# A decoder block on one core: sums, diagonals and transposes regrouped, the first values' weights loaded in halves, and another order of the end

## The chip, the cores and the metric

The kernel runs on one core of a Trainium2 chip. The metric is the device time of one execution in microseconds (us). Before the change three runs took 449.29, 447.87 and 447.54 us, a median of 447.87.

## The reference, cut to what matters

A block for 256 tokens of width 1024: a norm, one wide projection (latents of queries, 384, and of keys and values, 256; one rotary key; queries, keys and values of eight further heads; two gates), two attentions of eight heads, their merge, an output projection, a gated MLP with a convolution over three tokens, and a final norm.

```python
h = rmsnorm(x, attn_norm[l])
proj = h @ w_in[l]
q_lat, kv_lat, k_pe, qkv_b = ...
q = rmsnorm(q_lat, q_norm[l]) @ w_uq[l]
kv = rmsnorm(kv_lat, kv_norm[l]) @ w_ukv[l]
y_a = causal_attention_blocks(q_a, k_a, v_a, ...) @ w_o_mla[l]
y_b = moba_attention(rope(qkv[0], pos), rope(qkv[1], pos), qkv[2]) @ w_o_moba[l]
x = x + (g_a * y_a + g_b * y_b) @ w_out[l]
h = rmsnorm(x, ffn_norm[l])
u = causal_dwconv(h @ w_up[l], conv_w[l], conv_b[l])
x = x + (silu(u[..., :D_FF]) * u[..., D_FF:]) @ w_down[l]
return rmsnorm(x, final_norm)
```

## The kernel before, in words

**Products.** Every float32 operand of a large product is split into a high part (rounded to a shorter format, on ScalarE) and a low part (the rest, on VectorE), and a product is three: high times high, high times low, low times high (`mm3`, line 341; `split`, line 346). A few small products use plain float32: transposes against the identity, rows of a norm's factors, sums over partitions.

**Weights.** They come in units of 128 x 2048 (1 MB) in the order of `PLAN` (line 44). `weights` (line 353) takes the next of three raw tiles, three high and three low ones, loads the unit on SP's queue in one transfer, and splits it in two cuts of 1024 columns. A raw tile is loaded again when VectorE's subtraction has read it.

**Order.** All work is first recorded by `Program` (line 144) and then emitted by a list scheduler (`emit`, line 212): with prices per instruction (`price`, line 283) it goes on in model time, and each engine takes, of the instructions whose inputs are there, the one recorded first. SP takes its transfers strictly in recorded order. What is recorded inside `P.together()` stays in one block. So where a line stands in the program is its priority, and the order that comes out on each engine is fixed; on the chip each engine works it off in that order. From line 916 on VectorE, ScalarE and GpSimd keep the recorded order.

**Start.** Four units hold the tokens and the weights of the latents (line 510). Then the values' projection for the first 512 columns (`proj_tokens`, line 463; banks `v0`), while x is loaded again and its squares give the first norm's factor r1 (line 540, three small GpSimd operations with a power). `to_rows` (line 439) lays a factor per token out as a row in all partitions: VectorE multiplies the identity by the factor (a diagonal, from a ring of two tiles) and TensorE multiplies it by ones. `keep_values` (line 551) scales the values by r1. The second half of the values (banks `v1`, line 570) has the sums of the latents' squares (`lat_sums`, line 562) between its groups of products. Then the values' second half is kept, GpSimd works out the latents' factors `r_lat` (line 572), two `to_rows` lay them out, and the latents are scaled (line 584).

**Attentions.** Four units with two heads each of the one kind (line 663), then four of the other (line 724), with the gates' units between them. In `attention` (line 603): scores, maximum, exponentials with their sums, reciprocal; then for each head two scalings on ScalarE, three transposes in a block, a split of the transposed weights, and the products with the values.

**MLP and end.** `up_unit` (line 808) uses the second norm's factor, laid out by `to_rows` in the first unit (line 821). `down` (line 849) adds products into five banks (`parts`, line 842: for the first 128 tokens two halves of 512 columns, for the second 512, 256 and 256). The end (lines 916 to 933): `add` adds a bank to the residual and squares it on ScalarE into a column of `means`; `sum_up` adds these columns one by one, on GpSimd but for the last, which VectorE adds; `root` takes the power on GpSimd; `gains` multiplies by the final norm's weights on VectorE; `scaled` multiplies by the root in pieces and stores them, the last piece on ScalarE and its queue, the others on VectorE and SP's queue.

Of the kernel before, what the change touches and what calls it, by code (L numbers as in the profile page):

```python
# [27 lines left out]
D = 1024  # L28
# [278 lines left out]
def hybrid_block(ctx: ExitStack, tc: tile.TileContext, x, par, con, fnorm, wpack, out):  # L307
# [45 lines left out]
    def weights(kind, i, *cuts):  # L353
# [6 lines left out]
        sp.dma_start(raw[:, :n], wpack[u, :, :n])  # L360
# [76 lines left out]
    diag = Ring("diag", 2, [128])  # L437

    def to_rows(o, col2):

        for tt in range(2):
            dg = diag()
            dve.tensor_scalar(dg, ident, col2[:, tt : tt + 1], None, op0=ALU.mult)
            mm(o[:, 128 * tt : 128 * tt + 128], ones, dg, True, True, False)
# [18 lines left out]
    def proj_tokens(kind, i0, o, ah, al, *between):  # L463

        for part in range(2):
            wv = groups(weights(kind, i0 + part), 4, 512)
            for k4 in range(4):
# [6 lines left out]
                if k < len(between):  # L474
                    between[k]()
# [66 lines left out]

    rbc, c1, s1 = (T(t, [S]) for t in ("rbc", "c1", "s1"))
    p = sc_bank()
    to_rows(p[:, 0:S], r1)
# [14 lines left out]
    lat_ss = sc_bank()  # L560

    def lat_sums(j, tt):

        mm(lat_ss[:, 2 * j + tt : 2 * j + tt + 1], sq[:, 3 * j, 128 * tt : 128 * tt + 128],
           ones[:, 0:1], True, True)

    v1 = [mm_bank(), mm_bank()]
    for j, f in ((0, 1), (0, 2), (3, 4)):
        dve.tensor_add(sq[:, j], sq[:, j], sq[:, f])
    proj_tokens("v", 2, v1, xh, xl, *(partial(lat_sums, j, tt) for j in range(2) for tt in range(2)))  # L570
    keep_values(v1, 1)
# [8 lines left out]
    for j in range(2):  # L580
        to_rows(p[:, S * j : S * j + S], r_lat[:, 2 * j : 2 * j + 2])
# [18 lines left out]
    exps = T("e", [768])  # L600
    phs, pls = (Ring(t, 2, [384], F32R) for t in ("ph", "pl"))

    def attention(i, q, k, more, scale, vh, vl, yh, yl):
# [31 lines left out]
        o = av_bank()  # L635
        for hh in heads:
# [4 lines left out]
            p = sc_bank()  # L641
            with P.together():
                for b, t in enumerate((e[0][:, hh], e[1][:, hh, :128], e[1][:, hh, 128:])):
                    pe.transpose(p[:, 128 * b : 128 * b + 128], t, ident)
            ph, pl = phs(), pls()
            split(ph, pl, p[:, :384])
# [161 lines left out]
    def up_unit(i, ph, pl):  # L808
# [10 lines left out]
        if i == 0:  # L819
            p = sc_bank()  # L820
            to_rows(p[:, 0:S], r2)
            act.copy(rbc2, p[:, 0:S])
# [53 lines left out]
    def sum_up(engine, j, other):  # L876

        engine.tensor_scalar(means[:, j : j + 1], means[:, j : j + 1], other, None, op0=ALU.add)
# [4 lines left out]
    def scaled(tt, cuts):  # L883

        r = r3[:, tt : tt + 1]
        for q, (a, b) in enumerate(zip(cuts, cuts[1:])):
            if q < len(cuts) - 2:
# [81 lines left out]
```

## Time and profile before

| what | us |
|---|---|
| median of three runs | 447.87 |
| the profiled execution's own time | 447.01 |
| span of the profile, first to last instruction | 445.2 |
| TensorE busy | 435.9 |
| VectorE busy | 357.7 |
| ScalarE busy | 273.0 |
| GpSimd busy | 10.5 |

In the profile PE is TensorE, PEld its weight loads, DVE VectorE, ACT ScalarE, POOL GpSimd and SP the engine that issues most transfers (SPq, ACTq: the queues). Products overlap in TensorE's pipeline, so a product's own duration is longer than the distance of two starts. Nearly every instruction has line 246, where the program emits it, so instructions are told apart by tile: `mm`, `sc` and `av` are banks, `whi` and `wlo` the split weights, `smalls` the small columns, `B` the output tile at the end, `gate` the residual there (and, at the start, the latents), `tb` the scratch of the squares, `e` the exponentials.

### The profile page before, as it was taken

Reading aid. Unit: us, or ns where it says so; the run is one execution under the profiler, and the core shown is the slowest. Engines: PE = TensorE matmul, PEld = TensorE weight load, DVE = VectorE, ACT = ScalarE, POOL = GpSimd, SP = SyncE. Lnnn points to the kernel's source line nnn. Section 1 sums busy time; section 2 is a strip of 40 time slices with the busy share of each in tenths; the row PEclk is TensorE's granted clock in tenths of the full one; section 3 lists DMA queues with packets and bytes.
Section 4 is the critical chain, followed back from the end, with each engine's and each line's share of the span. In section 5 each row is a group of like instructions: output and inputs, shape, how many; then the busy total and the mean of one; then the engine's idle time right before and its main releaser. Section 6 shows DMA issues by size and latency. Waiting matters only on the chain.

```text
span 445.2 us, 8253 instructions
## 1 busy us (share of the span) xinstructions
PE 435.9 (98%) x3366; PEld 415.2 (93%) x3366; DVE 357.7 (80%) x553; ACT 273.0 (61%) x471; POOL 10.5 (2%) x25
## 2 busy tenths in 40 slices
PE   8999999999999999999999999999999999999993
PEld 6988999999999999999998899999999999999982
DVE  5669998798879886993788569998787797797765
ACT  5687547455735676788665658765565565565523
POOL 0012000000000000000000010000000000000003
PEclk9999999999999999999999999999999999999998
DMA  7986655435452443240479355386555555556002
GB/s 285 392 337 219 255 188 191 160 125 188 162 181 98 153 173 113 94 191 3 176 301 343 125 190 187 105 299 209 193 205 194 197 198 201 193 200 227 2 0 94
DMA packets 12997, 81.77 MB, mean 184 GB/s; under 512 B 1568, under 2 KB 2208, under 8 KB 4256
## 3 DMA queue, kind: packets, MB, share of 16 engines
q1 hardware_dynamic: 12528, 80.85, 50.4%
q8 instruction: 26, 0.43, 0.4%
q10 hardware_dynamic: 432, 0.40, 0.3%
q14 instruction: 11, 0.09, 0.1%
HBM read 80.20 MB, written 1.05 MB: 182 GB/s over the span
## 4 chain that ended last, share of the span: by engine, by line
PE 89%; DVE 4%; DMA 3%; ACT 1%; issue 1%; POOL 1%; SPq 0%; POOLq 0%; ACTq 0%; DVEq 0%
PE mm L246 63%; PE sc L246 13%; PE av L246 13%; DMA raw<-in_wpack 3%; DVE wlo L246 2%; POOL smalls L246 1%; DVE gate L246 1%; DVE VL L246 1%; ACT whi L246 0%; SPq L246 0%; DVE B L246 0%; ACT tb L246 0%; POOLq L964 0%; DVE tb L246 0%; ACT VH L246 0%
## 5 line engine op out<-in xcount | busy, mean ns | idle before, releaser
L246 DVE TENSOR_TENSOR wlo<-raw,whi 128x1024 fp32r<-128x1024 f32 (+4 forms) x155 | 175.7, 1147 | 36.1 <-ACT whi L246 35.6
L246 ACT CAST whi<-raw 128x1024 fp32r<-128x1024 f32 (+3 forms) x153 | 151.2, 1000 | 85.0 <-PE mm L246 65.7
L246 PE MATMUL mm<-XH,whi 128*128 128x256 f32 x656 | 176.9, 279 | 0.0
L246 PE MATMUL mm<-XL,whi 128*128 128x256 f32 x656 | 175.1, 277 | 0.0
L246 PE MATMUL mm<-XH,wlo 128*128 128x256 f32 x656 | 175.0, 276 | 0.0
L246 PEld LDWEIGHTS mm<-XH,whi 128*128 128x128 f32 x656 | 120.6, 188 | 1.1 <-ACT whi L246 0.6
L246 PEld LDWEIGHTS mm<-XL,whi 128*128 128x128 f32 x656 | 120.6, 188 | 0.4
L246 PEld LDWEIGHTS mm<-XH,wlo 128*128 128x128 f32 x656 | 120.4, 188 | 0.0
L246 DVE SCALAR_TENSOR_TENSOR tb<-ta,prm,tb 128x255 f32<-128x255 f32 x88 | 40.4, 480 | 2.2 <-ACT tb L246 0.7
L246 ACT ACTIVATE tb<-ta,prm 128x256 f32<-128x256 f32 x44 | 24.2, 594 | 3.8 <-DVE ta L246 3.8
L246 PE MATMUL sc<-whi,ql 128*128 128x512 f32 (+1 forms) x66 | 23.4, 355 | 0.0
L246 PE MATMUL sc<-wlo,qh 128*128 128x512 f32 (+1 forms) x66 | 23.3, 353 | 0.0
L246 PE MATMUL sc<-whi,qh 128*128 128x512 f32 (+1 forms) x66 | 23.1, 351 | 0.0
L246 ACT ACTIVATE e<-sc,smalls 128x128 f32<-128x128 f32 (+1 forms) x32 | 13.3, 420 | 12.8 <-DVE smalls L246 11.9
L246 ACT CAST qh<-ta 128x256 fp32r<-128x256 f32 (+1 forms) x26 | 11.3, 435 | 12.4 <-DVE ta L246 12.4
L246 DVE TENSOR_TENSOR ta<-ta,tb 128x256 f32<-128x256 f32 (+1 forms) x35 | 16.9, 484 | 2.2 <-ACT ta L246 0.7
L246 DVE TENSOR_TENSOR ta<-mm,rbc 128x512 f32<-128x512 f32 x22 | 15.2, 689 | 4.2 <-PE mm L246 4.2
L246 PE MATMUL mm<-YBH,whi 128*128 128x256 f32 x64 | 18.1, 283 | 0.0
L246 PE MATMUL mm<-YBH,wlo 128*128 128x256 f32 x64 | 17.7, 277 | 0.0
L246 PE MATMUL mm<-VH,whi 128*128 128x256 f32 x64 | 17.7, 277 | 0.0
L246 PE MATMUL mm<-YBL,whi 128*128 128x256 f32 x64 | 17.7, 277 | 0.0
L246 PE MATMUL mm<-VH,wlo 128*128 128x256 f32 x64 | 17.7, 276 | 0.0
(169 smaller groups left out, 741.8 us busy)
## 6 DMA issues: line engine op xcount, KB each, us to landing
raw<-in_wpack SPq DMA_DIRECT2D x66, 1024.0 KB, 4.8
raw<-in_wpack SPq DMA_DIRECT2D x7, 512.0 KB, 7.2
raw<-in_wpack SPq DMA_DIRECT2D x4, 832.0 KB, 4.2
B<-in_x SPq DMA_DIRECT2D x1, 1024.0 KB, 9.7
gate<-in_x SPq DMA_DIRECT2D x1, 1024.0 KB, 4.8
cst<-in_con SPq DMA_DIRECT2D x1, 641.0 KB, 10.7
raw<-in_wpack SPq DMA_DIRECT2D x2, 256.0 KB, 3.2
gate<-in_fnorm SPq DMA_DIRECT2D x1, 512.0 KB, 5.5
```

The costliest lines, as they stand in the source:

```text
L246: getattr(getattr(self.nc, e), method)(*args, **kw)
```

## The change

- `weights` can load a unit in several transfers. The first unit of the values is loaded in two halves and split in cuts that end at 512, 1024 and 2048.
- `to_rows` is divided: `to_diag` makes the diagonals, in six places of the tile of the exponentials (`exps`, allocated earlier) instead of a ring of two, and `to_rows` only multiplies them by ones.
- The sums of the latents' squares move from between the groups of the values' second half to one block with the rows of r1, ahead of them.
- All four diagonals of the latents' factors are multiplied in one block, recorded before the values' second half is kept. The second norm's two rows are in one block as well.
- In `attention` the transposes of both heads stand in one block behind all four scalings, and both splits come ahead of both products with the values.
- At the end all sums are GpSimd's. The last piece of the first 128 tokens is stored on SP's queue instead of ScalarE's. Of the second 128 tokens, columns 640 to 1024 and 0 to 256 are weighted ahead of the root; columns 256 to 640 get weight and root in one instruction.

```diff
--- before.py
+++ after.py
@@ -350,14 +349,16 @@
 
     units = iter(range(len(PLAN)))
 
-    def weights(kind, i, *cuts):
+    def weights(kind, i, *cuts, loads=1):
 
         u = next(units)
         assert PLAN[u] == (kind, i), (PLAN[u], kind, i)
         n = SIZE.get(kind, UNIT)
         raw, hi, lo = raws(), his(), los()
         cuts = cuts or (n // 2, n)
-        sp.dma_start(raw[:, :n], wpack[u, :, :n])
+        for j in range(loads):
+            c = slice(n * j // loads, n * (j + 1) // loads)
+            sp.dma_start(raw[:, c], wpack[u, :, c])
         a = 0
         for b in cuts:
             split(hi[:, a:b], lo[:, a:b], raw[:, a:b])
@@ -434,13 +435,20 @@
         used[0] += n
         return smalls[:, used[0] - n : used[0]]
 
-    diag = Ring("diag", 2, [128])
-
-    def to_rows(o, col2):
-
-        for tt in range(2):
-            dg = diag()
+
+    exps = T("e", [768])
+    diags = iter(exps[:, 128 * (j % 6) : 128 * (j % 6) + 128] for j in range(8))
+
+    def to_diag(col2):
+        dgs = [next(diags) for _ in range(2)]
+        for tt, dg in enumerate(dgs):
             dve.tensor_scalar(dg, ident, col2[:, tt : tt + 1], None, op0=ALU.mult)
+        return dgs
+
+    def to_rows(o, dgs):
+
+
+        for tt, dg in enumerate(dgs):
             mm(o[:, 128 * tt : 128 * tt + 128], ones, dg, True, True, False)
 
     def feature_tile(o, m, w, ah, al, ks, first, last):
@@ -460,10 +468,14 @@
                                  m == 0 and k == 0, k > 0)
         return o
 
-    def proj_tokens(kind, i0, o, ah, al, *between):
+    def proj_tokens(kind, i0, o, ah, al):
 
         for part in range(2):
-            wv = groups(weights(kind, i0 + part), 4, 512)
+            if (kind, i0, part) == ("v", 0, 0):
+                wv = weights(kind, 0, 512, 1024, 2048, loads=2)
+            else:
+                wv = weights(kind, i0 + part)
+            wv = groups(wv, 4, 512)
             for k4 in range(4):
                 k = 4 * part + k4
                 with P.together():
@@ -471,8 +483,6 @@
                         c = slice(128 * tt, 128 * tt + 128)
                         mm3(o[tt], ah[:, k, c], al[:, k, c], wv[0][:, 0, k4], wv[1][:, 0, k4],
                             k == 0, k == KT - 1)
-                if k < len(between):
-                    between[k]()
 
     def two(ap):
         return ap[:, None, :].to_broadcast([ap.shape[0], 2, S])
@@ -540,9 +550,18 @@
     rsqrt(r1, ss[:, 0:2], D, 2)
     pool.tensor_tensor(r1sq, r1, r1, op=ALU.mult)
 
+    for j, f in ((0, 1), (0, 2), (3, 4)):
+        dve.tensor_add(sq[:, j], sq[:, j], sq[:, f])
     rbc, c1, s1 = (T(t, [S]) for t in ("rbc", "c1", "s1"))
-    p = sc_bank()
-    to_rows(p[:, 0:S], r1)
+    p, lat_ss = sc_bank(), sc_bank()
+    dgs = to_diag(r1)
+    with P.together():
+        for j in range(2):
+            for tt in range(2):
+
+                mm(lat_ss[:, 2 * j + tt : 2 * j + tt + 1],
+                   sq[:, 3 * j, 128 * tt : 128 * tt + 128], ones[:, 0:1], True, True)
+        to_rows(p[:, 0:S], dgs)
     act.copy(rbc, p[:, 0:S])
     dve.tensor_mul(lat[:, 5], lat2[:, S:], rbc)
     dve.tensor_mul(c1, cos1, rbc)
@@ -557,18 +576,8 @@
 
     keep_values(v0, 0)
 
-    lat_ss = sc_bank()
-
-    def lat_sums(j, tt):
-
-        mm(lat_ss[:, 2 * j + tt : 2 * j + tt + 1], sq[:, 3 * j, 128 * tt : 128 * tt + 128],
-           ones[:, 0:1], True, True)
-
     v1 = [mm_bank(), mm_bank()]
-    for j, f in ((0, 1), (0, 2), (3, 4)):
-        dve.tensor_add(sq[:, j], sq[:, j], sq[:, f])
-    proj_tokens("v", 2, v1, xh, xl, *(partial(lat_sums, j, tt) for j in range(2) for tt in range(2)))
-    keep_values(v1, 1)
+    proj_tokens("v", 2, v1, xh, xl)
     r_lat = small(4)
     for j, n in enumerate((QL, KVL)):
         c = slice(2 * j, 2 * j + 2)
@@ -577,8 +586,11 @@
         rsqrt(r_lat[:, c], t, n, 2)
         pool.tensor_tensor(r_lat[:, c], r_lat[:, c], r1, op=ALU.mult)
     p = sc_bank()
-    for j in range(2):
-        to_rows(p[:, S * j : S * j + S], r_lat[:, 2 * j : 2 * j + 2])
+    dgs = [to_diag(r_lat[:, 2 * j : 2 * j + 2]) for j in range(2)]
+    with P.together():
+        for j in range(2):
+            to_rows(p[:, S * j : S * j + S], dgs[j])
+    keep_values(v1, 1)
     lt = T("LT", [2, 5, S], F32R)
     lth, ltl = lt[:, 0], lt[:, 1]
     for f in range(5):
@@ -597,7 +609,6 @@
                                  op0=ALU.mult, op1=ALU.subtract)
 
 
-    exps = T("e", [768])
     phs, pls = (Ring(t, 2, [384], F32R) for t in ("ph", "pl"))
 
     def attention(i, q, k, more, scale, vh, vl, yh, yl):
@@ -632,18 +643,22 @@
                 act.activation(e[qt][:, hh], views[qt][:, hh], AF.Exp, bias=nm[:, j : j + 1],
                                scale=scale, accum_out=sm[:, j : j + 1])
         dve.reciprocal(rs, sm)
-        o = av_bank()
         for hh in heads:
             for qt in range(2):
                 j = 2 * qt + hh
                 act.activation(e[qt][:, hh], e[qt][:, hh], AF.Copy, scale=rs[:, j : j + 1])
 
-            p = sc_bank()
-            with P.together():
+        p = [sc_bank() for _ in heads]
+        with P.together():
+            for hh in heads:
                 for b, t in enumerate((e[0][:, hh], e[1][:, hh, :128], e[1][:, hh, 128:])):
-                    pe.transpose(p[:, 128 * b : 128 * b + 128], t, ident)
-            ph, pl = phs(), pls()
-            split(ph, pl, p[:, :384])
+                    pe.transpose(p[hh][:, 128 * b : 128 * b + 128], t, ident)
+        pv = [(phs(), pls()) for _ in heads]
+        for hh in heads:
+            split(*pv[hh], p[hh][:, :384])
+        o = av_bank()
+        for hh in heads:
+            ph, pl = pv[hh]
             r = o[:, S * hh : S * hh + S]
             c = slice(128 * (2 * i + hh), 128 * (2 * i + hh) + 128)
             with P.together():
@@ -818,7 +833,9 @@
                              m == 0 and k == 0, k > 0)
         if i == 0:
             p = sc_bank()
-            to_rows(p[:, 0:S], r2)
+            dgs = to_diag(r2)
+            with P.together():
+                to_rows(p[:, 0:S], dgs)
             act.copy(rbc2, p[:, 0:S])
         us, ac = tas(), tbs()
 
@@ -873,23 +890,26 @@
     def gains(tt, a, b):
         dve.tensor_mul(y[:, tt, a:b], x2[:, tt, a:b], fn[:, a:b])
 
-    def sum_up(engine, j, other):
-
-        engine.tensor_scalar(means[:, j : j + 1], means[:, j : j + 1], other, None, op0=ALU.add)
+    def sum_up(j, other):
+
+        pool.tensor_scalar(means[:, j : j + 1], means[:, j : j + 1], other, None, op0=ALU.add)
 
     def root(tt, j):
         pool.tensor_tensor(r3[:, tt : tt + 1], means[:, j : j + 1], mhalf[:, 0:1], op=ALU.pow)
 
-    def scaled(tt, cuts):
+    def scaled(tt, cuts, queue):
 
         r = r3[:, tt : tt + 1]
         for q, (a, b) in enumerate(zip(cuts, cuts[1:])):
-            if q < len(cuts) - 2:
-                dve.tensor_scalar(y[:, tt, a:b], y[:, tt, a:b], r, None, op0=ALU.mult)
-                sp.dma_start(out[:, tt, a:b], y[:, tt, a:b])
+            piece = y[:, tt, a:b]
+            if q == len(cuts) - 2:
+                act.activation(piece, piece, AF.Copy, scale=r)
+            elif q == 1:
+                dve.scalar_tensor_tensor(piece, x2[:, tt, a:b], r, fn[:, a:b], op0=ALU.mult,
+                                         op1=ALU.mult)
             else:
-                act.activation(y[:, tt, a:b], y[:, tt, a:b], AF.Copy, scale=r)
-                act.dma_start(out[:, tt, a:b], y[:, tt, a:b])
+                dve.tensor_scalar(piece, piece, r, None, op0=ALU.mult)
+            (queue if q == len(cuts) - 2 else sp).dma_start(out[:, tt, a:b], piece)
 
     prods = []
     for g in range(FT // 2):
@@ -915,22 +935,22 @@
                 product(j, k)
     P.in_order = ("vector", "scalar", "gpsimd")
     add(0)
-    sum_up(pool, 0, EPS)
+    sum_up(0, EPS)
     add(1)
     gains(0, 0, D)
-    sum_up(pool, 1, means[:, 0:1])
+    sum_up(1, means[:, 0:1])
     root(0, 1)
     add(2)
-    scaled(0, (0, 640, D))
-    sum_up(pool, 2, EPS)
+    scaled(0, (0, 640, D), sp)
+    sum_up(2, EPS)
     add(3)
-    sum_up(pool, 3, means[:, 2:3])
+    sum_up(3, means[:, 2:3])
     add(4)
-    gains(1, 0, 512)
-    sum_up(dve, 4, means[:, 3:4])
+    gains(1, 640, D)
+    gains(1, 0, 256)
+    sum_up(4, means[:, 3:4])
     root(1, 4)
-    gains(1, 512, D)
-    scaled(1, (0, 256, 640, D))
+    scaled(1, (0, 256, 640, D), act)
     P.emit()
 
 
```

## Rows read from the trace of the kernel before

**Rows 1.** Windows: us, busy time (instructions) of each engine, granted clock, DMA share, GB/s.

```profile
49.50:69.00 19.50, 19.50 (x173) 19.50 (x174) 19.34 (x25) 8.80 (x10) 0.00 (x0) 1.00 0.56 194
...
437.80:445.20 7.40, 0.02 (x1) 0.00 (x0) 3.06 (x8) 2.04 (x7) 1.52 (x3) 0.80 0.38 142
...
sum 445.20, PE 435.90 PEld 415.20 DVE 357.66 ACT 272.98 POOL 10.49; mean PE 31.14 PEld 29.66 DVE 25.55 ACT 19.50 POOL 0.75
```

**Rows 2.** Chain of waits, in order of time: start, us, what.

```profile
75.93 0.33 PE sc L246 x3
...
206.80 0.66 PE sc L246 x6
...
233.36 10.99 PE av L246 x48
```

**Rows 3.** Timeline near 20 us: start, us, engine, line, operation [idle before, releaser].

```profile
19.82 2.00 ACT L246 CAST whi<-raw 128x1024 fp32r<-128x1024 f32 x2 [3.65 <-DMA raw<-in_wpack]
...
21.59 0.39 PE L246 MATMUL av<-whi,XH 128*128 128x512 f32 x1
...
22.18 0.50 PE L246 MATMUL av<-wlo,XH 128*128 128x512 f32 x1 [0.20 <-DVE wlo L246]
...
22.52 0.39 PE L246 MATMUL av<-whi,XL 128*128 128x512 f32 x1
```

**Rows 4.** Timeline of TensorE around the two blocks of the latents' diagonals.

```profile
45.45 0.61 PE L246 MATMUL sc<-diag,ones 128*128 128x128 f32 x4
...
48.52 0.28 PE L246 MATMUL mm<-XH,wlo 128*128 128x256 f32 x1
...
49.34 0.71 PE L246 MATMUL sc<-diag,ones 128*128 128x128 f32 x4 [0.54 <-DVE diag L246]
```

**Rows 5.** Timeline of TensorE at the first of the latents' four sums.

```profile
34.90 0.28 PE L246 MATMUL sc<-ones,gate 128*128 128x1 f32 x2
...
35.36 0.40 PE L246 MATMUL mm<-wlo,XH 128*128 128x512 f32 x1
```

**Rows 6.** Timeline of GpSimd and VectorE ahead of these diagonals.

```profile
41.11 1.16 POOL L246 TENSOR_SCALAR smalls<-smalls 128x2 f32<-128x2 f32 x1 [10.83 <-DVE smalls L246]
...
42.14 0.48 DVE L246 SCALAR_TENSOR_TENSOR krl<-ta,cst,krh 128x256 fp32r<-128x256 f32 x1
...
43.49 0.48 DVE L246 TENSOR_SCALAR diag<-cst,smalls 128x128 f32<-128x128 f32 x2 [0.87 <-POOL smalls L246]
...
44.99 0.57 POOL L246 TENSOR_TENSOR smalls<-smalls 128x2 f32<-128x2 f32 x1
```

**Rows 7.** Timeline at the first attention's scores.

```profile
67.68 0.68 DVE L246 TENSOR_TENSOR kl<-ta,kh 128x512 fp32r<-128x512 f32 x1
...
69.00 0.28 PE L246 MATMUL sc<-kl,qh 128*128 128x128 f32 x1
```

**Rows 8.** Timeline of ScalarE: the four scalings of the first attention.

```profile
74.31 1.50 ACT L246 ACTIVATE e<-e,smalls 128x128 f32<-128x128 f32 x4
```

**Rows 9.** Timeline of the end.

```profile
436.94 0.57 POOL L246 TENSOR_TENSOR smalls<-smalls,mhalf 128x1 f32<-128x1 f32 x1
...
438.35 0.36 ACTq L246 DMA_DIRECT2D out<-B  x1
...
438.75 0.42 ACT L246 ACTIVATE tb<-gate 128x256 f32<-128x256 f32 x1 [0.44 <-DVE gate L246]
...
439.43 0.28 POOL L246 TENSOR_SCALAR smalls<-smalls 128x1 f32<-128x1 f32 x1 [1.25 <-ACT tb L246]
...
439.90 0.68 DVE L246 TENSOR_TENSOR B<-gate 128x512 f32<-128x512 f32 x1
...
440.06 0.95 POOL L246 TENSOR_TENSOR smalls<-smalls,mhalf 128x1 f32<-128x1 f32 x1 [0.35 <-DVE smalls L246]
...
441.05 0.68 DVE L246 TENSOR_SCALAR B<-B,smalls 128x256 f32<-128x256 f32 x2 [0.47 <-POOL smalls L246]
...
441.87 0.38 SPq L246 DMA_DIRECT2D out<-B  x1
```

More of the change, by code (lines that the diff above doesn't have):

```diff
@@ L11 @@
 from contextlib import ExitStack, contextmanager
-from functools import partial
 import numpy as np
```

## The prediction

> **What bounds the kernel now.** I read the windows first: TensorE is busy for 435.90 of 445.20 us, and in the 7.40 us behind its last product it does nothing while VectorE, ScalarE and GpSimd finish the norm and the stores [rows 1]. So the time is TensorE's stream plus a tail, and a change can only win where that stream has a hole, where an instruction in it gets cheaper, or in the tail. The chain of waits says the same: long pieces of TensorE in which 48 products of 512 columns last 10.99 us, 0.229 us each; a product of 256 columns takes about half, 0.114 [rows 2]. I then went along TensorE's timeline for starts that come later than these slots allow. Behind the warm-up and the first loads, which the change leaves alone, two holes remain: the start of the values' projection [rows 3] and a wait for a diagonal in the middle of the first query unit [rows 4]. Last I looked at who feeds TensorE next: VectorE, busy 19.34 of 19.50 us between 49.5 and 69 [rows 1], is the engine that could give the gain back.
>
> **The values' first weights** (two loads, cuts at 512, 1024, 2048). Now the 1 MB piece is waited for until 19.82, cast and subtracted in pieces of 1024 columns, and TensorE, there at 21.59, gets its second product at 22.18 and the third at 22.52 [rows 3]. Lost: (0.59 - 0.229) + (0.34 - 0.229) = 0.47 us. From the cast's start to the release is 22.18 - 19.82 = 2.36 us; for half the columns an estimate is 1.2 to 1.4, so the first piece is ready at 21.2 even if its load lands no earlier, and TensorE asks at 21.82. The hole goes: -0.47, with 0 as the other bound (the second cut of 512 then being late by as much, though it is needed six products later). SP issues one load more; it waits for released buffers afterwards, which hides it.
>
> **The latents' sums** (four one-column products, now one behind each of four groups of the second values' projection). Each moves the second product behind it to 35.36 - 34.90 - 0.229 = 0.23 us later [rows 5], 0.92 in all. Moved into one block with r1's diagonals they are still executed. What does a switch of kind cost? Transposes answer: three alone last 0.33 us, six in one block 0.66 [rows 2], so nothing. I take 0.1 for all regrouped blocks together (sums, diagonals of both norms, transposes); the bounds are 0 and 0.46, half of the sums' price. In the new block the sums stand ahead of r1's rows, which so come 0.9 us later; ScalarE's copy of them and the casts queued behind it shift by that. What hides it is the first half of the projection, some 5.5 us of products on weights that are ready; with that cover gone it would cost the 0.9.
>
> **The diagonals of the latents' norms.** Now there are two blocks of two products, at 45.45 and at 49.34. Before the second, TensorE stands from 48.52 + 0.114 to 49.34, 0.71 us, and that block then lasts 0.71 instead of 0.61 [rows 4]: 0.81 us. The wait is for VectorE, and that is late because GpSimd's six small operations on the sums run from 41.11 to 45.56 [rows 6], and then three subtractions and two values stand ahead. After the change the last sum stands ahead of the projection, four groups of 6 x 0.229 us and four sums earlier, which is 6.4 us; the six operations end before 41 even at the length they have now, the diagonals have six tiles instead of a ring of two, and all four products stand in one block at the end of the projection (near 45). The values of the second half move behind it. The hole goes: -0.81. If the planner still puts the block ahead of its diagonals, 0.
>
> **What may be late next.** VectorE's queue is full from 33 to 68. The first score block needs the key's low part: the subtraction starts at 67.68, lasts 0.68, and its product starts at 69.00 [rows 7], so 0.64 us are left, say 0.5 with the hand-over. TensorE would now come 0.47 + 0.81 + 0.1 = 1.38 us earlier. VectorE comes earlier by the 0.47 of its values' wait, and by the 0.87 us that it now idles for GpSimd ahead of a diagonal at 43.49 [rows 6], if the new diagonals make it wait less. If that wait vanishes nothing is lost; if it stays as long, 1.38 - 0.47 - 0.5 = 0.4 is. I take 0.2 back.
>
> **The transposes of both heads in one block.** In four of the eight attentions they already stand so (six in a row [rows 2]); in the other four the first head's transposes now wait for all four scalings on ScalarE instead of two: 1.50 us for four [rows 8], so 0.75 later. Ahead of them in TensorE's order stand products of other units; 0 while these last, at most 0.75 each.
>
> **The end.** (a) The store of the first half's last piece leaves ScalarE's queue, where its issue takes 0.36 us at 438.35, for SP's, which has nothing else there until the stores behind the last root; the squares behind it start at 438.75 [rows 9] and could at 438.47, as soon as the residual sum is there: -0.28 for both squares. (b) GpSimd adds the last sum itself. Now its root waits 0.35 us for VectorE [rows 9]. Then: second squares 0.42 behind the first, 0.68 from a square's start to GpSimd's start (438.75 to 439.43), so 438.47 + 0.42 + 0.68 = 439.57, plus 0.28 for the sum: root at about 439.9, against 440.06. (c) 640 columns are weighted ahead instead of 1024. Now 512 of them run at 439.90 on VectorE beside the root, which takes 0.95 us; the first root took 0.57 [rows 9]. The 640 can start when the second squares do (438.47 + 0.42 = 438.89, both behind the last residual sum) and take some 0.85 (512 take 0.68), so they end at 439.7, before the root begins, and I take 0.57: root done at 440.5 instead of 441.01, 0.5 earlier; 0.15 earlier with the slow root. The Trainium skill (SBUF — State Buffer, Who interferes with whom) says that a VectorE instruction with two SBUF inputs and a GpSimd one that reads SBUF exclude each other for a whole instruction; by that rule the weighting lengthened the root, and the sum here comes out the same. (d) The other 384 columns get weight and scale in one instruction: VectorE's two pieces of 256 and 384 take 0.68 now [rows 9], and a scalar_tensor_tensor of 256 takes 0.48 [rows 6], so 384 about 0.7, and the last store, issued 0.86 behind the root (441.87), comes up to 0.3 later. The two stores ahead of it may hide that. I take 0.1. End: -0.4, between +0.15 and -0.5.
>
> **Sum**: -0.47 - 0.1 - 0.81 + 0.2 - 0.4 = -1.6 us. The profiled execution took 447.01 us, 0.86 under the median of the runs shown (447.87); on the median 1.6 gives 446.3 us, -0.35%. A measurement of this kernel tells about 0.5% (2.2 us) from no change.
>
> **Rivals.**
> *VectorE keeps the gain.* GpSimd's six operations take 4.45 us, while the planner prices them near 1.9 (lines 299 and 300). The diagonals now stand in VectorE's order where the planner thinks they are ready, up to 2.6 us too early, and values, rope tables and weights queue behind them. Then VectorE is 2.6 - 0.87 - 0.47 = 1.3 later, the scores of the first attention wait 1.38 + 1.3 - 0.5 = 2.2, and with -1.38 and -0.4 elsewhere the sum is +0.4: 448.3. For it: the 0.87 wait. Against: GpSimd's operations of 0.2 us last that long where VectorE works beside them. Half of it gives 447.2. By the rule of the Trainium skill above the lengthening goes away where VectorE reads only one operand from SBUF, as in the values; that would leave 446.3. Chance 0.2.
> *Slower: merged transposes starve TensorE.* Place: the four attentions now split. Price up to 4 x 0.75 = 3.0 us; from 0.4 us each it eats the 1.6. Time 447.87 - 1.6 + 3.0 = 449.3. Against: four attentions already run merged, and TensorE has no hole there. Chance 0.1.
> *The planner's order leaves the hole at 49.* Then only the values' start and the end count: 447.0. Chance 0.1.
> *All bounds at best*: 0.47 + 0.46 + 0.81 + 0.5 = 2.2, which gives 445.6. For it: every term has a row. Against: VectorE's full queue. Chance 0.2.
>
> **Numbers.** The forecast, 446.3, has 0.4. The range goes from 445.0 (best bounds, less 0.6 for the spread of the runs, 447.54 to 449.29) to 448.4 (the first rival); it leaves out the transposes and part of the spread. Faster by over 0.5% (under 445.6): 0.24, half of the last rival's chance and a third of the forecast's by that spread. Slower by over 0.5% (over 450.1): 0.06, half of the transposes' chance with a second hole beside theirs. Within: 0.70.
>
> **What would show it.** Right: the values' second product 0.23 behind the first near 21.8; one block of four sums and two diagonals near 33 and one of four diagonals near 45; no idle TensorE between 45 and 70; the tail near 6.9 instead of 7.40; the last root near 0.57. Wrong: idle TensorE before the scores near 68 or before transposes, VectorE waiting over 1.5 us for GpSimd between 34 and 41, or a last store that lands no earlier. The forecast fails if TensorE's busy time itself shrinks by over 1 us, since then a switch of kind has a price after all.

## The result and the profile after

The changed kernel took 452.84 us (median of four runs, 451.90 to 455.08) where the kernel before took 448.16 beside it: a ratio of 1.0118, 95% interval 1.009 to 1.0145. The forecast was 446.3 us in a range of 445.0 to 448.4. The change makes the kernel 1.2% slower, and none of the terms of the sum, nor any rival, was large enough for that.

The page of the changed kernel begins with its span and TensorE's busy time (share, instructions):

```profile
span 451.1 us, 8263 instructions
...
PE 441.6 (98%) x3366; PEld 421.2 (93%) x3366; DVE 358.5 (79%) x553; ACT 272.7 (60%) x472; POOL 9.6 (2%) x26
```

The span is 5.9 us longer and TensorE is busy 5.7 us longer than before [rows 1], with the same products to compute. I set the starts of the same products in the two traces side by side. The second column is the profile shown here, the third another execution of the same kernel (the repeat among the experiments):

| product that before starts at | after minus before, us | in the repeat |
|---|---|---|
| 21.59 (values' first product) | +1.05 | -0.10 |
| 49.81 (behind the diagonals) | +0.01 | -1.36 |
| 214.16 (last attention's output) | -0.34 | -0.80 |
| 216.20 | +1.40 | +0.95 |
| 265.52 (first behind the second norm's rows) | +1.39 | +0.93 |
| 437.54 (last product) | +6.11 | +5.65 |
| end of the span | +5.92 | +5.46 |

So the gains forecast for the first 50 us came (1.04 and 1.26 us), as did a little at the end. Two losses stand against them: 1.74 us in one place near 214 us, and 4.7 us spread evenly from 266 us to the end. The 1.05 us at the start are not the change's, since the repeat has -0.10 there; without them the span would be 4.9 us longer, near the 4.7 us between the medians.

**The even loss.** The chain of waits from the first up unit on (start, us, what, how many; a full-precision product of 128 columns stands as two instructions, and a piece starts where the one ahead ends, while the table has the products' own starts). Before:

```profile
261.22 0.22 PE sc L246 x2
261.44 4.10 PE mm L246 x36
265.54 0.22 PE sc L246 x2
265.76 13.62 PE mm L246 x120
...
284.86 10.91 PE mm L246 x96
```

After:

```profile
261.25 5.46 PE mm L245 x48
266.70 0.45 PE sc L245 x4
267.15 14.14 PE mm L245 x120
...
286.82 11.31 PE mm L245 x96
```

Ahead of the second norm's rows a product lasts 113.7 to 113.9 ns in both kernels (5.46 us for 48, 4.10 for 36). Behind the two rows in one block the same 120 products take 14.14 instead of 13.62 us, 117.8 ns instead of 113.5 from start to start, and the 96 of each later unit 11.31 instead of 10.91. I call these the long and the short pace. The granted clock is 1.00 in both stretches, and TensorE is busy throughout, as the windows from 270 to 281 us say (columns as in [rows 1]; before, then after):

```profile
270.00:281.00 11.00, 11.00 (x94) 10.84 (x94) 9.82 (x20) 9.49 (x15) 0.00 (x0) 1.00 0.45 168
270.00:281.00 11.00, 11.00 (x95) 11.00 (x95) 9.74 (x18) 9.21 (x15) 0.00 (x0) 1.00 0.51 186
```

**The single loss.** The timeline of ScalarE and TensorE near 214 us after (start, us, engine, line, operation, idle before and its releaser):

```profile
205.37 1.28 ACT L245 ACT_TABLE_LOAD   x1
206.67 0.51 ACT L245 ACTIVATE gate<-gate,prm 128x256 f32<-128x256 f32 x1
207.08 1.48 ACT L245 ACTIVATE e<-e,smalls 128x128 f32<-128x128 f32 x4
...
211.34 0.83 ACT L245 CAST ph<-sc 128x384 fp32r<-128x384 f32 x2
...
212.07 2.91 ACT L245 ACTIVATE gate<-gate,prm 128x256 f32<-128x256 f32 x7
...
214.45 0.28 PE L245 MATMUL mm<-VH,wlo 128*128 128x256 f32 x1
214.88 0.57 ACT L245 CAST VH<-av 128x512 fp32r<-128x512 f32 x1
...
215.50 0.38 PE L245 MATMUL mm<-VH,whi 128*128 128x256 f32 x1 [0.77 <-ACT VH L245]
216.23 0.39 PE L245 MATMUL mm<-VL,whi 128*128 128x256 f32 x1 [0.34 <-DVE VL L245]
```

ScalarE's timeline there before:

```profile
204.60 1.49 ACT L246 ACTIVATE e<-e,smalls 128x128 f32<-128x128 f32 x4
206.11 1.28 ACT L246 ACT_TABLE_LOAD   x1
...
208.62 0.83 ACT L246 CAST ph<-sc 128x384 fp32r<-128x384 f32 x2
...
212.64 0.57 ACT L246 CAST VH<-av 128x512 fp32r<-128x512 f32 x1
```

In the last attention the planner now puts the table load and a gate's sigmoid ahead of the four scalings, and seven sigmoids in all ahead of the two casts `ph`, where three stood before. The output `VH` is cast 2.24 us later, and TensorE, whose next product needs it and its low part `VL`, gets one product done between 214.45 and 216.23.

**What came as forecast.** TensorE's timeline after, for the values' start, the block of the sums and the block of four diagonals:

```profile
22.64 0.40 PE L245 MATMUL av<-whi,XH 128*128 128x512 f32 x1
22.88 0.40 PE L245 MATMUL av<-wlo,XH 128*128 128x512 f32 x1
...
33.84 0.95 PE L245 MATMUL sc<-ones,gate 128*128 128x1 f32 x8
34.65 0.69 PE L245 MATMUL sc<-e,ones 128*128 128x128 f32 x4
...
46.19 1.05 PE L245 MATMUL sc<-e,ones 128*128 128x128 f32 x8
47.00 0.37 PE L245 MATMUL mm<-XH,whi 128*128 128x256 f32 x1
```

The second value product stands 0.24 us behind the first, not 0.59 [rows 3]; four sums in a row take 34.65 - 33.84 = 0.81 us instead of 4 x 0.23 [rows 5]; the four diagonals take 0.81, with no wait ahead [rows 4]. GpSimd's timeline at the end after:

```profile
445.24 0.93 POOL L245 TENSOR_SCALAR smalls<-smalls 128x1 f32<-128x1 f32 x2 [1.02 <-ACT tb L245]
446.25 0.58 POOL L245 TENSOR_TENSOR smalls<-smalls,mhalf 128x1 f32<-128x1 f32 x1
```

The last root takes 0.58 us, not 0.95 [rows 9], as forecast; but the two sums ahead of it take 0.93 where two took 0.28 each on GpSimd.

### The profile page after: what moved, and what is told of

It reads as the page before. It is cut to its first block, busy times and chain, and to the rows that moved or that the text cites. A ratio compares the mean times of both kernels' runs of the same rounds, so it can differ in the third digit from the quotient of the medians.

```text
span 451.1 us, 8263 instructions
## 1 busy us (share of the span) xinstructions
PE 441.6 (98%) x3366; PEld 421.2 (93%) x3366; DVE 358.5 (79%) x553; ACT 272.7 (60%) x472; POOL 9.6 (2%) x26
## 3 DMA queue, kind: packets, MB, share of 16 engines
HBM read 80.20 MB, written 1.05 MB: 180 GB/s over the span
## 4 chain that ended last, share of the span: by engine, by line
PE 94%; ACT 3%; DVE 1%; POOL 1%; issue 0%; POOLq 0%; DVEq 0%; ACTq 0%
PE mm L245 68%; PE sc L245 13%; PE av L245 13%; ACT gate L245 1%; POOL smalls L245 1%; ACT e L245 1%; ACT L245 0%; ACT tb L245 0%; ACT B L245 0%; DVE gate L245 0%; DVE B L245 0%; ACT ph L245 0%; DVE VL L245 0%; POOLq L984 0%; DVEq L984 0%
## 5 line engine op out<-in xcount | busy, mean ns | idle before, releaser
L245 ACT CAST whi<-raw 128x1024 fp32r<-128x1024 f32 (+4 forms) x154 | 151.5, 994 | 92.6 <-PE mm L245 72.1
L245 PE MATMUL mm<-XL,whi 128*128 128x256 f32 x656 | 177.2, 280 | 0.0
L245 PE MATMUL mm<-XH,wlo 128*128 128x256 f32 x656 | 177.1, 280 | 0.0
L245 PEld LDWEIGHTS mm<-XH,wlo 128*128 128x128 f32 x656 | 122.1, 190 | 0.0
L245 PE MATMUL mm<-VL,whi 128*128 128x256 f32 x64 | 17.8, 278 | 0.3 <-DVE VL L245 0.3
```

The costliest lines, as they stand in the source:

```text
L245: getattr(getattr(self.nc, e), method)(*args, **kw)
```

## The experiments

Each ran beside the kernel before on the same chip; its median there was 447.55 us for the first four runs, 447.37, 447.57 and 447.61 for the later sets. The theory: the joined rows of the second norm start the long pace, and the joined transposes change ScalarE's order at the last attention. First each part was undone alone, or done alone.

**The second norm's rows apart** in the changed kernel:

```diff
-            dgs = to_diag(r2)
-            with P.together():
-                to_rows(p[:, 0:S], dgs)
+            for tt in range(2):
+                dg = next(diags)
+                dve.tensor_scalar(dg, ident, r2[:, tt : tt + 1], None, op0=ALU.mult)
+                mm(p[:, 128 * tt : 128 * tt + 128], ones, dg, True, True, False)
```

> The changed kernel with one part undone: the second norm's two rows (line 836) are again two blocks of one product each. Theory (the joined block starts the slow pace): the 256-column products of the feed-forward half start 113.4 ns apart again instead of 117.7, some 4.6 us come back, and the time is about 448.2. Rival (the pace has another cause: addresses, an earlier block, or chance): the products stay near 117.7 ns behind 266 us and the time stays near 452.8.

Measured: 448.52 us, ratio 1.0025 (1.0012 to 1.0038), and 13.62 us for the 120 products. Some 4 us come back. In the chain of waits, behind the second row:

```profile
267.39 13.62 PE mm L245 x120
```

What is left is the wait at 214 us and, behind that wait, the long pace up to a block of eight transposes at 249 us (against before, the products come 0.69 us later at 216 us and 1.63 at 261).

**The transposes apart** in the changed kernel:

```diff
-        p = [sc_bank() for _ in heads]
-        with P.together():
-            for hh in heads:
+            p = sc_bank()
+            with P.together():
                 for b, t in enumerate(...):
-                    pe.transpose(p[hh][...], t, ident)
+                    pe.transpose(p[...], t, ident)
...
```

> The changed kernel with one part undone: each head's transposes, split and value products follow its own scalings, as before. Theory (the joined transposes let ScalarE put a table load and sigmoids ahead of the last attention's work): the wait of TensorE near 214.5 us, about 1.6 us, is gone, and the time is about 451.2, with the slow pace behind 266 us unchanged. Rival (the joined transposes also set the pace): the products start 113.4 ns apart behind 266 us and the time is near 446.7.

Measured: 451.23 us, ratio 1.0086 (1.0066 to 1.0106). TensorE is busy for all of the 12 us from 205 to 217, against 10.89 in the changed kernel; the long pace behind 266 us is still there.

**The joined rows alone** in the kernel before:

```diff
-            to_rows(p[:, 0:S], r2)
+            dgs = [diag() for _ in range(2)]
+            for tt, dg in enumerate(dgs):
+                dve.tensor_scalar(dg, ident, r2[:, tt : tt + 1], None, op0=ALU.mult)
+            with P.together():
+                for tt, dg in enumerate(dgs):
+                    mm(p[:, 128 * tt : 128 * tt + 128], ones, dg, True, True, False)
```

> The kernel before with one part of the change alone: the second norm's two diagonals and rows in one block. Theory (the joined block starts the slow pace): 117.7 ns between the starts of the 256-column products from that block to the end, about 4.6 us more, so 452.5. Rival (the pace needs the other parts too, or is chance): 113.4 ns and about 448.

Measured: 451.63 us, ratio 1.0093 (1.0074 to 1.0111), and 14.14 us for the 120 products. The chain of waits, behind the block:

```profile
265.70 14.14 PE mm L246 x120
```

From 23 to 261 us every product stands within 0.1 us of its place before; the 36 products that had stood between the two rows come 0.29 us earlier, and the last product comes 4.66 us later (4.1 by the medians). The joined block does it by itself.

**The joined transposes alone** in the kernel before (the edit of the second run the other way round):

```diff
+        p = [sc_bank() for _ in heads]
+        with P.together():
+            for hh in heads:
...
```

> The kernel before with one part of the change alone: both heads' transposes in one block, both splits, then the value products. Theory (ScalarE's order at the last attention makes the wait): a wait of TensorE of about 1.6 us near 215 us and a time about 1.5 us longer, 449.6, with the products at 113.4 ns. Rival 1 (the order comes from other parts): no wait, about 448. Rival 2 (the joined transposes also slow the pace): 117.7 ns behind 266 us, about 454.

Measured: 449.07 us, ratio 1.0040 (1.0023 to 1.0057). The wait is there with the same releasers; the products gain 0.25 us up to 146 us and lose 1.75 near 215. The pace stays short behind 266 us.

**Both parts undone** in the changed kernel (the first two edits together):

```diff
-            with P.together():
-                to_rows(p[:, 0:S], dgs)
+                mm(p[:, 128 * tt : 128 * tt + 128], ones, dg, True, True, False)
...
```

> The changed kernel with the second norm's two rows apart and each head's transposes on their own, as before: what is left of the change is the values' first weights, the latents' block, the block of four diagonals and the end. Theory (these parts give what was forecast, and the two undone parts made all of the loss): 113.4 ns between the products behind 266 us, no wait near 214 us, and 1.2 to 1.6 us under the kernel before (near 446.3). Rival (the remaining parts also shift the pace or the start): at or above the kernel before.

Measured: 446.89 us, ratio 0.9983 (0.9970 to 0.9997): under the kernel before, but by 0.5 us and not by 1.2 to 1.6. The wait for VectorE and the pace of the first stage, both below, each take some 0.6 us of an execution in which they occur; how much of the rest they make up is not shown.

**The last four attentions apart only**, as the next candidate:

```diff
+        apart = more is not None
...
+            if apart:
+                with P.together():
+                    turned(hh)
+                pair(hh)
+                value(hh)
```

> As the run with both parts undone, but in the first four attentions both heads' transposes stay in one block; only in the last four does each head go on its own. Theory (joined blocks of six transposes keep the fast pace where blocks of three lose it for some 2 us, and only the last attention has ScalarE's changed order): 0.2 to 0.3 us under the run with both undone. Rival (the joining costs a wait somewhere in the first four): over it.

Measured: 446.53 us, ratio 0.9978 (0.9966 to 0.9990). The difference from the run before it has the right sign and is inside the intervals; not settled.

**The front alone**, with rows, attentions and end as before:

```diff
-    gains(1, 640, D)
-    gains(1, 0, 256)
-    sum_up(4, means[:, 3:4])
+    gains(1, 0, 512)
+    sum_up(dve, 4, means[:, 3:4])
...
```

> The kernel before with the values' first weights, the latents' block and the block of four diagonals alone; the end, the second norm's rows and the attentions as before. Theory: the holes at 22 and 49 us are gone, TensorE's products stand some 1.2 us earlier from 50 us to the end, the tail stays at 7.4 us: 1.0 to 1.2 us under the kernel before, 0.2 to 0.4 over the run with both undone. Rival (VectorE's queue takes the gain back before the first scores): the products from 70 us on stand within 0.4 us of those of before.

Measured: 445.81 us, ratio 0.9967 (0.9957 to 0.9977). The products stand 1.26 us earlier from 69 us to the last one, and the tail is 7.5 us. That it is faster than the run with the new end as well was not expected.

**Three rows in the block**, to see what about the block matters:

```diff
                 to_rows(p[:, 0:S], dgs)
+                mm(p[:, S : S + 128], ones, dgs[1], True, True, False)
```

> The changed kernel with a third product (a repeat of the second row into unused columns) in the second norm's block. Theory 1 (how many products a block has decides which pace follows; blocks of three transposes in a row kept or lost it, blocks of six always kept it): the block of three is followed by 113.4 ns, and the time falls by 4.6 less 0.1 us to about 448.3. Theory 2 (any block of more than one full-precision product in the middle of this stream starts the slow pace): 117.7 ns, about 452.9.

Measured: 448.64 us, ratio 1.0034 (1.0021 to 1.0047). One more product makes the kernel 4 us faster. The chain of waits of this run:

```profile
261.10 5.46 PE mm L245 x48
266.56 0.67 PE sc L245 x6
267.23 13.62 PE mm L245 x120
```

**A lone product later**, behind the joined block:

```diff
+        if i == 2:
+            mm(sc_bank()[:, 0:128], ones, rbc2[:, 0:128], True, True, False)
```

> The changed kernel with one more full-precision product of 128 columns on its own (its result unused) some 70 products behind the second norm's joined block. Theory 1 (the pace holds itself until the next full-precision block, and what that block is decides anew; lone products were followed by 113.4 ns each time): 117.7 ns from 266 us to the lone product near 275, 113.4 behind it, and some 448.7 us. Theory 2 (once slow, the stream stays slow whatever full-precision work stands in it): 117.7 ns to the end, about 452.9.

Measured: 448.97 us, ratio 1.0029 (1.0015 to 1.0043). The chain of waits:

```profile
267.89 0.45 PE sc L245 x4
268.33 8.48 PE mm L245 x72
276.82 0.22 PE sc L245 x2
277.04 5.46 PE mm L245 x48
```

72 products at 117.8 ns behind the block of two, then, behind the lone product, 113.7 ns to the end. The pace holds itself up to the lone product and is short behind it.

**Four rows in the block:**

```diff
+                for c in (S, S + 128):
+                    mm(p[:, c : c + 128], ones, dgs[1], True, True, False)
```

> The changed kernel with four products in the second norm's block (two repeats into unused columns). Theory 1 (an even count starts the slow pace, an odd one doesn't): 117.7 ns behind the block, about 453. Theory 2 (two is the only count seen that does; longer blocks don't): 113.4 ns, about 448.5.

Measured, one time: 453.89 us. The chain of waits:

```profile
267.23 0.89 PE sc L245 x8
268.12 14.14 PE mm L245 x120
```

One and three are followed by the short pace, two and four by the long one. Three and four were profiled once each; the ten runs with three, from 448.04 to 449.96, all lie under every run of the changed kernel.

**A better end**, on the version with the last four attentions apart:

```diff
     add(2)
+    gains(1, 0, 256)
     scaled(0, (0, 640, D), sp)
...
     gains(1, 640, D)
-    gains(1, 0, 256)
```

> As the run with the last four attentions apart, but at the end the weighting of the second half's first 256 columns stands in VectorE's idle time ahead of the first half's scaling, so that only 384 columns are weighted behind the last residual sum. Theory (in the new end VectorE's two-operand weighting lengthens GpSimd's last sum from 0.28 to over 0.6 us, instead of the root as before): the last sum takes near 0.28, the root begins some 0.3 us earlier, the tail behind TensorE's last product is near 7.0 us instead of 7.3. Rival (the sum is long by itself): the tail stays at 7.3.

Measured: 445.77 us, ratio 0.9961 (0.9946 to 0.9976). GpSimd's timeline at its end:

```profile
439.21 0.68 POOL L245 TENSOR_SCALAR smalls<-smalls 128x1 f32<-128x1 f32 x2 [1.03 <-ACT tb L245]
439.97 0.58 POOL L245 TENSOR_TENSOR smalls<-smalls,mhalf 128x1 f32<-128x1 f32 x1
```

The two sums last 0.68 us together instead of 0.93, and the tail is 7.05 us. It was the first of the two that had been long, 0.55 us, not the last as the expectation said.

**The changed kernel again**, without an edit:

> The changed kernel once more. If the slow pace behind 266 us belongs to the kernel, it is there again at 117.7 ns, with the wait near 214.5 us, and the ratio is near 1.011. If the 1.05 us by which the values' first product came later is chance of the start, that product moves by some tenths of a microsecond; if it belongs to the kernel, it is again near 22.6 us with 118 ns in the first stage.

Measured: 452.53 us, ratio 1.0110 (1.0097 to 1.0123). The long pace and the wait at 214 us are there again. The values' first product starts at 21.49, so the 1.05 us at the start were chance of one execution. Some 0.6 us of them (144 products by 4.1 ns) are the pace again: from 5 to 20 us, in the latents' products, it is 117.8 ns in the first profile and 113.7 in this one, at a granted clock of 1.00 in both. The front alone shows the same in its two profiles (113.5 here, 117.8 when it ran again). Of all 18 profiles seven have the long pace in all or most of this stage, so one kernel can have either from one execution to the next.

This trace also has a wait that the first had not. Its timeline on the way to the first scores (VectorE, GpSimd, TensorE):

```profile
40.11 1.22 DVE L245 TENSOR_TENSOR wlo<-raw,whi 128x1024 fp32r<-128x1024 f32 x1
40.13 1.75 POOL L245 TENSOR_TENSOR smalls<-smalls,mhalf 128x2 f32<-128x2 f32 x1
...
42.18 0.48 DVE L245 TENSOR_SCALAR e<-cst,smalls 128x128 f32<-128x128 f32 x2 [0.86 <-POOL smalls L245]
...
68.15 0.33 PE L245 MATMUL sc<-kl,qh 128*128 128x128 f32 x1 [0.44 <-DVE kl L245]
```

In the run with the front alone the power starts ahead of the subtraction instead of behind it; its timeline there:

```profile
39.98 0.69 POOL L245 TENSOR_TENSOR smalls<-smalls,mhalf 128x2 f32<-128x2 f32 x1
40.18 1.21 DVE L245 TENSOR_TENSOR wlo<-raw,whi 128x1024 fp32r<-128x1024 f32 x1
...
41.48 0.48 DVE L245 TENSOR_SCALAR e<-cst,smalls 128x128 f32<-128x128 f32 x2
```

With the power 1.75 us long VectorE waits 0.86 us for the second diagonals, is that much later at the key's low part, and TensorE's first scores come 0.6 us later; with 0.7 to 0.8 us nothing of this happens. Of the 14 profiles with the block of four diagonals, eight have the long power and TensorE's wait, six neither.

**Four more runs settle the end's term.** The end alone, in the kernel before:

```diff
+    gains(1, 640, D)
+    gains(1, 0, 256)
+    sum_up(4, means[:, 3:4])
...
```

> The kernel before with the new end alone. Theory (the end is worth what its traces show): the tail behind TensorE's last product is 7.2 to 7.3 us instead of 7.4 to 7.5, and the time is 0.1 to 0.3 us under the kernel before. Rival (the new end costs, as the medians of the run with both parts undone, 446.9, and of the run with the front alone, 445.8, would have it): 0.5 us or more over the kernel before.

Measured: 446.99 us, ratio 0.9990 (0.9977 to 1.0002); the tail is 7.19 us, 0.22 shorter than before. No cost; a gain too small for the medians.

The front alone again, and both parts undone again (no new edit):

> The run with the front alone once more, as a measure of how far one kernel's median moves between two sets of executions. If the medians hold, it is again 1.5 us under the kernel before, near 445.9; if they move with how many executions have GpSimd's long power ahead of the second diagonals and the wait of 0.6 us behind it, it lies between 445.8 and 446.5.

> The run with both parts undone once more. If the new end is a gain, it is 0.1 to 0.3 us under the run with the front alone of the same set; if it is a loss, again some 1 us over it, near 446.9.

Measured: 446.00 us, ratio 0.9964 (0.9951 to 0.9976), and 446.77 us, ratio 0.9982 (0.9971 to 0.9992). The medians hold. Of the two profiles of the kernel with both parts undone the first has no wait at the first scores; the second has the long power and loses 0.65 us there. Both profiles of the front alone have the short one. So the 0.8 to 1.1 us between the two kernels are not in the end, whose tail is 0.2 us shorter in the slower one; that its executions have the long power more often fits, but was seen in two profiles each and is not shown for the rest. The pace of the first stage was long in one profile of each kernel (most of that stage in the kernel with both parts undone), so how often it is long is another candidate.

Both parts undone with the better end:

```diff
     add(2)
+    gains(1, 0, 256)
...
-    gains(1, 0, 256)
```

> Both parts undone, and the weighting of the second half's first 256 columns moved into VectorE's idle time, without any joined transposes. Theory: GpSimd's sums take 0.28 to 0.30 us each, the tail is near 7.05 us, and the time is 0.2 to 0.3 us under the run with both parts undone of the same set, 445.5 to 446.0. Rival (executions scatter by more than the tail is worth): no difference to it beyond the intervals.

Measured: 446.58 us, ratio 0.9978 (0.9968 to 0.9989); tail 7.05 us, and the profile has the long power. Against 446.77 the intervals overlap: the tail's gain is shown by the traces, not by the medians.

**The version to keep** is the front alone (0.9967 and 0.9964 in two sets) or the one with the better end and the last four attentions apart (0.9961): both beat the kernel before and the changed one, and nothing here tells them apart.

## Why the prediction was wrong

**The step that failed** is the question "What does a switch of kind cost?" and its answer "so nothing", with 0.1 for all regrouped blocks and bounds of 0 and 0.46. The bounds priced the blocks themselves, and there they hold: the sums gave 0.11, the joined transposes of the first half 0.25. They left out what a block does to the products behind it. One of the regrouped blocks, the second norm's two rows, put the products of the whole MLP on the long pace: 4.7 us in the trace of the run that has this edit alone, 4.1 by its median. The kernel before held a sign of it that I did not read. In its chain of waits, behind the block of three transposes whose duration I did take [rows 2], and behind the next one:

```profile
76.26 1.39 PE mm L246 x12
77.64 0.33 PE sc L246 x3
77.97 1.42 PE mm L246 x12
79.39 0.64 PE av L246 x6
80.03 1.42 PE mm L246 x12
```

Twelve products last 1.39 us behind the first block and 1.42 behind the second. Without the first two distances the median from start to start is 114 ns behind the one and 118 behind the other, and 113 to 114 against 118 in all four attentions that stood apart. The pace was already not one number; the sum divided 10.99 us by 48 and took half of it for every product of 256 columns.

**The merged transposes** were right in their sign for the first attentions and wrong in their bound for the last. "At most 0.75 each" priced the two scalings that now stand ahead of the first head's transposes. The cost, 1.74 us, came from the planner: with the transposes later in the program, the table load and a sigmoid went ahead of its scalings, and four more sigmoids (seven instead of three) and a copy ahead of its two casts. The place was the last attention, whose six transposes stood together already before [rows 2] and where I had costed nothing. The rival had the right engine waiting on an attention, but neither this place nor this cause.

**The values' first weights** (forecast -0.47): the hole is gone, in the repeat -0.36 us at the second product and 0.1 more at the third. **The diagonals** (-0.81): the wait and the slower block are gone; with the sums, the front gives 1.26 us between 21.59 and 49.81 where 1.38 were forecast.

**VectorE late at the first scores** (+0.2): it is 0 or 0.6, by whether GpSimd's second power starts ahead of VectorE's subtraction or behind it, a difference of 0.2 us between executions; the 0.2 forecast is neither. This is the first rival in its place and by its mechanism, at 0.6 us instead of its 2.2. A rule of the Trainium skill speaks of it (SBUF — State Buffer, Who interferes with whom): VectorE's second SBUF input and GpSimd's reads share a port, and one of the two waits for a whole instruction. The traces agree: 0.69 us when GpSimd goes first, 1.75 when a subtraction of 1.22 us does.

**The end** (-0.4): -0.19 in both profiles of the changed kernel, -0.22 with the end alone, and -0.09 to -0.19 in the other profiles that have this end, against a tail of 7.41 us before. The squares start 0.63 us behind the end of the last product instead of 0.93, near the 0.28 forecast. The root is short, as forecast. But the work that lengthened it was only moved, beside the sums, one of which became 0.27 us longer. The run with the better end gets this back, for a tail 0.36 us under that of before.

What was named as a sign of failure, that TensorE's busy time "shrinks by over 1 us", points the wrong way: it grew by 5.7.

## What to carry to other kernels

A small block inside a long stream is priced by what the stream does behind it, too: divide the length of a run of equal products by their count on both sides of each block, and compare kernels by that quotient, since no wait and no clock row shows it. When a list planner orders an engine, moving work later in the program also moves other work ahead of it, so look at the order that comes out for every engine before costing a regrouping. And an operation on GpSimd of some tenths of a microsecond can grow by about the length of the VectorE instruction that starts just ahead of it: here a power of 0.69 us took 1.75 behind a subtraction of 1.22.

## What the runs showed of the hardware

Products of 256 columns behind one another have two paces at the same granted clock of 1.00 (of the two levels the upper one, 2.4 GHz): 113.4 and 117.8 ns from start to start. In the MLP each holds itself over hundreds of products, through weight changes and runs of nine products of 512 columns, which last the same in either, 229 ns each. Two longer runs of 512 columns behind products at the long pace took 233.3 ns each instead of 228.9: the values' first half in the first profile of the changed kernel, and 60 products from 235 us on in the run with the rows apart.

At the second norm, blocks of one and of three products with the diagonals were followed by the short pace each time, blocks of two and four by the long one, in every profile of either kind. This is no rule for every block. An even count was followed by the short pace near 46 us, behind products of 512 columns, and at 49 us, behind a wait of 0.54 us [rows 4]. Where the heads' transposes stand apart, the first block of three was followed by the short pace and the second by the long one in every attention; the blocks of eight transposes near 260 us were followed by the short one. And the first stage, with no such block in it, had either pace.

Why the count decides at the second norm stays open, and so does what sets the pace behind a wait: behind the one at 214 us it was short in both profiles of the changed kernel, and long up to 249 us in the runs with the rows apart and with four products. The Trainium skill (TensorE: Matmul & The Clock Gate, Wait — 56ns, not 53.3ns?) gives one distance for back-to-back products at full clock, the columns' time and 2.5 ns more. That would be 109 ns here, an estimate from the page's figures; the runs show neither that nor one value, and the measurement decides.
